# A two-block transformer kernel: the layout of on-chip memory, and short two-byte products behind the norms

## The chip, the cores and the metric

The kernel runs on one core of a Trainium2 chip. The metric is the device time of one launch in microseconds (us). A core has a matrix engine (PE, whose weight loads the profile lists apart as PEld), a vector engine (DVE), an activation engine (ACT), GpSimd (POOL) and a queue engine (SP) that here only issues transfers. All of them read and write one on-chip memory of 128 partitions. An address below is an offset inside a partition, in KiB; it is the same in every partition and comes from the built program.

A PE product has a stationary operand, loaded first, and a moving operand that streams past it. In the rows "128*128 128x256" is a product whose moving operand has 256 columns.

## The reference

256 tokens of width 1024 pass through two blocks, in float32:

```python
# block 1
h = rms_norm(x, g_mix); z = h @ w_in
x = x + concat(mla(...), hgrn2(...)) @ w_o
h = rms_norm(x, g_ffn)
x = x + (silu(h @ w_gate) * (h @ w_up)) @ w_down        # inner width 2816
x = x + sigmoid(rms_norm(x, g_ple) @ w_ple_gate) * (p @ w_ple_proj)
# block 2
proj = rms_norm(x, norm_mix_g) @ w_in_2                 # qa ka va qb kb vb f g_a g_b
ya = moba_attention(...) @ w_branch_a
yb = forgetting_attention(...) @ w_branch_b
x = x + (sigmoid(g_a) * ya + sigmoid(g_b) * yb) @ w_out
qh = rms_norm(x, norm_ffn_g) @ w_peer_q                 # 8 heads, two halves of 128
s = qh @ sub_keys; take the best 16 of 128 in each half, the best 16 of the 256 pairs, softmax
x = x + sum over the chosen of gate * gelu(h . expert_u[e]) * expert_v[e]   # 16384 experts
out = rms_norm(x, norm_final_g)
```

## The kernel before, in words

Activations lie transposed, features on partitions and 256 tokens along the row, in eight slices of 128 features. PE's accuracy on its fast float32r type does not do for float32, so every large product is made three times: an operand is split into a rounded part and a remainder (hh and hl for activations, whi and wlo for weights), and hi·hi, lo·hi and hi·lo are added up in PSUM. `mm3s` (L120 to L131) issues them for products that keep features on partitions: weights stationary, activations moving, 256 columns, all by the PE call of L129. `natural` (L163) does it with activations stationary and weights moving, 512 columns, for the projections that are wanted with tokens on partitions.

`unit` (L99 to L118) brings weights in: SP starts the transfer of a 512 KB piece into `wraw` (L108), ACT rounds it to `whi` (L109), DVE takes the difference `wlo` (L114). Each has four buffers.

A norm is spread over the products that follow it. Class `Norm` splits the unscaled residual times the gain into hh and hl, and `make` returns two steps that are placed between products: `sums` (L230 to L237) adds the squares of a token over the partitions by true float32 products against `ones` and has DVE (L197, tile nv) and POOL (L198, tile rnat) make the root; `spread` (L239 to L244) puts the root, by two more float32 products (L241), across the partitions, and ACT copies it to rbc. The results of the products are multiplied by it later. Where the products are 128 wide and the weights come in units, a step stands behind a unit's 24 products.

In block 2 the products `whole` (L1063) multiply 18 groups of 128 experts in true float32 straight from `wraw`, with `xf`, the normed activations, moving. The one-hot products (L1227) that turn chosen experts into a table of gates are float16, 128 columns, sixteen in a row. The last stage runs over 128 groups c of 128 experts: `prepare` brings in expert_v (whi, wlo), multiplies the hidden value by the gate (tile am) and splits it into `ah` and `al`; `multiply` (L1252) issues 12 products of 512 columns per group with ah or al stationary and whi or wlo moving, into four accumulators. While c is below 64 the hidden values of later groups (`experts_in`, L1066, 24 products of L129 each) run in between. Behind group 127 `final` adds the residual, squares, and scales the result per half j of the tokens.

Tiles come from pools. A name has a fixed number of buffers, and names of one pool lie one behind the other in the order of first use, so that the pools `res` (hh, hl, xa, xb, rnat, rbc) and `st` (wraw, whi, wlo, sq, sqa, nv) fill the memory from its low end, and pools of a stage come above them. PE's order is the program's order but for instructions that the scheduler may move; what follows is taken from the built program.

## Time and profile before

| | us |
|---|---|
| median of 3 runs | 1409.96 |
| lowest, highest | 1408.98, 1412.89 |
| the profiled execution | 1412.48 |
| span of the profiled execution (first to last instruction) | 1410.7 |

The span is cut into 40 slices, and PE is at 9 tenths or more in all but the last (7 tenths). PE's granted clock is 0.8 of full speed in the second slice and in the last, and 0.9 or more in all others. Transfers take 8 tenths of the DMA engines' time at most in a slice, 196 GB/s on the mean.

A view with a row for a group of instructions gives their count, the sum of their times and the mean time of one. Products on PE overlap: the next one starts before the last has ended, so the mean time of one is longer than the distance from start to start. That distance, called the pitch below, is what a product costs in a row of products. It is had from a stretch in which PE never stopped: the length of the stretch plus one duration, divided by the number of products in it.

### The profile page before, as it was taken

The numbers are of one execution on the slowest core, as the hardware profiler recorded it, in microseconds if no ns is written. First come the engines' busy times: TensorE is split into PE (matmuls) and PEld (weight loads), VectorE is DVE, ScalarE is ACT, GpSimd is POOL, SyncE is SP. The second block draws the span as 40 slices with busy tenths as digits, with TensorE's granted clock in tenths as the row PEclk, the third lists the DMA queues.
The fourth block names the chain that finished last, engine by engine and source line by source line (L and its number), as shares of the span: only waits on it lengthen the run. The fifth ranks groups of instructions, "written<-read, shape, count | busy, mean of one in ns | idle before, by whom it ended". The sixth has DMA issues, their size and how long they took to land.

```text
span 1410.7 us, 25321 instructions
## 1 busy us (share of the span) xinstructions
PE 1390.7 (99%) x9970; PEld 1275.8 (90%) x9970; DVE 966.8 (69%) x1794; ACT 766.5 (54%) x1183; POOL 127.0 (9%) x117
## 2 busy tenths in 40 slices
PE   9999999999999999999999999999999999999997
PEld 9896999999989889999999999999989989888885
DVE  7867876665675556897989975555555555577775
ACT  6765655444654444573368885554444444445443
POOL 4322100000110000147200000000000000000000
PEclk9899999999999999999999999999999999999998
DMA  8572566566555334676478779667767767787662
GB/s 244 163 190 62 162 197 187 187 180 187 176 165 153 117 120 135 196 212 189 134 235 285 275 271 297 210 214 211 224 194 222 219 210 227 225 278 237 196 192 77
DMA packets 104999, 276.99 MB, mean 196 GB/s; under 512 B 8496, under 2 KB 42032, under 8 KB 102704
## 3 DMA queue, kind: packets, MB, share of 16 engines
q1 hardware_dynamic: 100848, 252.31, 57.6%
q10 hardware_dynamic: 2304, 16.78, 2.9%
q0 software_dynamic: 1728, 6.29, 2.5%
q8 instruction: 78, 1.28, 0.4%
q14 instruction: 41, 0.34, 0.1%
HBM read 251.23 MB, written 17.83 MB: 191 GB/s over the span
## 4 chain that ended last, share of the span: by engine, by line
PE 91%; DVE 4%; ACT 2%; DMA 2%; issue 1%; POOL 1%; SPq 0%; POOLq 0%; ACTq 0%; DVEq 0%
PE mm L129 50%; PE ax L1252 25%; PE mm L163 4%; PE ax L1227 2%; PE mm L1063 1%; DVE wlo L114 1%; PE sc L923 1%; ACT whi L109 1%; PE sc L129 1%; PE ao L917 1%; PE ay L163 1%; DMA wraw<-in_expert_v_dram 1%; PE ax L1038 1%; DVE hl L186 0%; DMA wraw<-in_expert_u_dram 0%
## 5 line engine op out<-in xcount | busy, mean ns | idle before, releaser
L109 ACT ACTIVATE whi<-wraw 128x1024 fp32r<-128x1024 f32 (+3 forms) x446 | 457.4, 1031 | 471.1 <-PE mm L129 249.4
L114 DVE TENSOR_TENSOR wlo<-wraw,whi 128x1024 fp32r<-128x1024 f32 (+3 forms) x412 | 489.0, 1190 | 253.2 <-ACT whi L109 243.7
L129 PE MATMUL mm<-hh,whi 128*128 128x256 f32 x1920 | 278.4, 283 | 1.1 <-ACT hh L185 0.4
L129 PE MATMUL mm<-hl,whi 128*128 128x256 f32 x1920 | 268.7, 278 | 0.9 <-DVE hl L186 0.8
L129 PE MATMUL mm<-hh,wlo 128*128 128x256 f32 x1920 | 267.2, 278 | 0.2 <-DVE wlo L114 0.2
L129 PEld LDWEIGHTS mm<-hh,whi 128*128 128x128 f32 x1920 | 249.4, 188 | 9.1 <-issue 0.9
L129 PEld LDWEIGHTS mm<-hl,whi 128*128 128x128 f32 x1920 | 241.6, 188 | 2.3 <-DVE hl L186 2.1
L129 PEld LDWEIGHTS mm<-hh,wlo 128*128 128x128 f32 x1920 | 241.3, 188 | 0.5 <-DVE wlo L114 0.3
L1252 PE MATMUL ax<-whi,al 128*128 128x512 f32 x512 | 201.2, 396 | 0.0
L1252 PE MATMUL ax<-wlo,ah 128*128 128x512 f32 x512 | 200.5, 395 | 0.0
L1252 PE MATMUL ax<-whi,ah 128*128 128x512 f32 x512 | 200.4, 395 | 0.0
L1252 PEld LDWEIGHTS ax<-whi,ah 128*128 128x128 f32 x512 | 96.2, 188 | 22.0
L1252 PEld LDWEIGHTS ax<-wlo,ah 128*128 128x128 f32 x512 | 96.3, 188 | 21.2
L1252 PEld LDWEIGHTS ax<-whi,al 128*128 128x128 f32 x512 | 96.2, 188 | 20.6 <-DVE al L181 0.4
L1068 ACT ACTIVATE hs<-mm 128x256 f32<-128x256 f32 x128 | 47.4, 371 | 40.1 <-PE mm L129 25.8
L1267 POOL TENSOR_TENSOR ff<-fss 128x1 f32<-128x1 f32 x2 | 1.4, 698 | 718.9 <-ACT fsq L1262 718.9
L114 POOL TENSOR_TENSOR wlo<-wraw,whi 128x1024 fp32r<-128x1024 f32 x22 | 52.5, 2397 | 24.9 <-ACT whi L109 22.9
L180 ACT ACTIVATE ah<-am 128x256 fp32r<-128x256 f32 x128 | 51.5, 402 | 4.4 <-DVE am L1243 4.4
L181 DVE TENSOR_TENSOR al<-am,ah 128x256 fp32r<-128x256 f32 x128 | 53.3, 418 | 0.0
L786 DVE TENSOR_TENSOR gu<-mm,rbc 128x256 f32<-128x256 f32 x44 | 18.6, 424 | 39.4 <-PE mm L129 39.4
L1217 DVE TENSOR_TENSOR one<-iota,iab 128x2048 f16<-128x2048 f16 x32 | 39.1, 1220 | 4.1 <-PE ax L1227 4.1
L1220 DVE TENSOR_TENSOR oA<-one,g 128x2048 f16<-128x2048 f16 x32 | 39.1, 1225 | 1.0
(407 smaller groups left out, 1552.4 us busy)
## 6 DMA issues: line engine op xcount, KB each, us to landing
wraw<-in_expert_u_dram SPq DMA_DIRECT2D x128, 512.0 KB, 4.5
wraw<-in_expert_v_dram SPq DMA_DIRECT2D x128, 512.0 KB, 3.9
wraw<-in_w_gu_dram SPq DMA_DIRECT2D x44, 512.0 KB, 3.5
wraw<-in_w_in_nat_dram SPq DMA_DIRECT2D x24, 512.0 KB, 3.7
wraw<-in_w_down_dram SPq DMA_DIRECT2D x16, 512.0 KB, 3.5
wraw<-in_w_in_g_dram SPq DMA_DIRECT2D x16, 512.0 KB, 3.5
wraw<-in_w_pq_dram SPq DMA_DIRECT2D x16, 512.0 KB, 4.4
gd<-hh ACTq DMA_DIRECT2D x8, 1024.0 KB, 6.8
```

Source lines behind the costliest of these rows:

```text
L109: S.activation(hi[:, s], raw[:, s], AF.Copy)
L114: (G if pool else V).tensor_tensor(lo[:, s], raw[:, s], hi[:, s].bitcast(F32), op=OP.subtract)
L129: PE.matmul(o, (wh, wl, wh)[j], (xh, xh, xl)[j], start=first and n == 0, stop=last and n == len(order) - 1)
L163: PE.matmul(p, xs[:, x0 + k, s], w[:, k], start=first and i == 0 and k == 0, stop=last and i == 2 and k == kts - 1)
L180: S.activation(hi, src, AF.Copy)
L181: V.tensor_tensor(lo, src, hi.bitcast(F32), op=OP.subtract)
L786: V.tensor_tensor(t, o, n1.r, op=OP.mult)
L1068: S.activation(t, p[:, :T], AF.Gelu)
L1217: V.tensor_tensor(one, iota[:, None].to_broadcast(s2), iab[:, qs].rearrange("p q w b -> p (q w) b")[:, :, None].to_broadcast(s2), op=OP.is ...
L1220: V.tensor_tensor(A2, ow[:, :, 0:1].to_broadcast(s3), g2[:, qs].rearrange("p q k b -> p (q k) b")[:, :, None].to_broadcast([128, PAIRS * 2 ...
L1227: PE.matmul(p[:, i * 128:(i + 1) * 128], ow[:, q, 1, b::2], A2[:, q, k, b::2], start=k == 0, stop=k == 1)
L1252: PE.matmul(acc[j * 2 + n], (al, ah, ah)[i][:, j * 128:(j + 1) * 128], (hi, lo, hi)[i][:, n * 512:(n + 1) * 512], start=c == 0 and i == 0, ...
```

## The change

**Layout.** Two pools, `reh` and `sth`, are laid from the high end of the memory. The residual streams xa and xb, the roots rnat and rbc, the raw weights wraw, the squares and nv go there. So the split activations and weights move down, and with them everything above. `ah` and `al` become slices of one tile in a buffer of `hl` that is free by then, and the odd ones of the gate tiles `gt`, which used hl, get a tile of their own. In KiB of a partition, from the built programs:

| tile (use on PE) | before | after |
|---|---|---|
| hh (moving in L129, stationary in L163) | 27.9 to 43.9 | 20.1 to 36.1 |
| hl (the same) | 43.9 to 59.9 | 36.1 to 52.1 |
| whi (stationary in L129, moving in L163, L1252) | 85.9 to 101.9 | 52.1 to 68.1 |
| wlo (the same) | 101.9 to 117.9 | 68.1 to 84.1 |
| act high and low, moving in w_down | 122 to 166 | 84.1 to 128 |
| oT, moving in w_branch | 156 to 172 | 118 to 134 |
| ah, al (stationary in L1252) | 210 to 218 | 44.1 to 52.1 |
| xf, moving in L1063 | 124 to 132 | 86 to 94 |
| float16 one-hots (L1227) | 198 to 214 | 160 to 176 |
| wraw, stationary in L1063 | 69.9 to 85.9 | 185.8 to 201.8 |
| keys in xa's place, moving in L1038 | 19.9 up | 205.9 up |
| xb's place, stationary in a few products of L163 | 59.9 up | 213.9 up |

**Two-byte products.** `level` issues one bfloat16 product of 128 columns on a tile of ones, into a region of PSUM that nothing reads. It stands seven times in the program: behind `spread` in each of five norms, once in w_down behind the first 24 products, and once behind the products `whole`.

**A spread moved.** In the first block of w_in_2 the step `spread` stands one group of products later.

**The end.** In `final`, the sum, scaling and epsilon of the two halves' squares go from POOL to DVE, POOL keeps the power alone, and the two additions of the residual for the last half come behind one another.

```diff
+    reh = pool("reh", side="right")
+    sth = pool("sth", side="right")
...
-        raw = st.tile([128, 1024], F32, name="wraw", bufs=4)
+        raw = sth.tile([128, 1024], F32, name="wraw", bufs=4)
...
-                sq = st.tile([128, T], F32, name="sq", bufs=2)
+                sq = sth.tile([128, T], F32, name="sq", bufs=2)
...
             def spread():
                 for j in range(2):
                     PE.matmul(self.p[:, T + j * 128:T + (j + 1) * 128], self.rn[:, j:j + 1].to_broadcast([128, 128]), ident,
                               start=True, stop=True)
-                self.r = res.tile([128, T], F32, name="rbc", bufs=2)
+                level(self.p[:, 0:128])
+                self.r = reh.tile([128, T], F32, name="rbc", bufs=2)
                 S.activation(self.r, self.p[:, T:], AF.Copy)
...
-    xa = lambda: res.tile([128, 8, T], F32, name="xa")
-    xb = lambda: res.tile([128, 8, T], F32, name="xb")
+    xa = lambda: reh.tile([128, 8, T], F32, name="xa")
+    xb = lambda: reh.tile([128, 8, T], F32, name="xb")
...
+    onesb = con.tile([128, 128], BF16, name="onesb")
+    G.memset(onesb, 1.0)
+
+    def level(p):
+
+        tc.keep_in_program_order(PE.matmul(p, onesb, onesb, start=True, stop=True))
...
                      n == 0 and k1 == 22, first=k0 == 0, last=k1 == 22)
+                if n == 0 and k0 == 0:
+                    level(pfx()[:, 0:128])
...
-        nat512("w_in2_nat", 0, h, emit_nat("qa"), pre=[lambda: None] + nb.make(ppt), behind=nb.last)
+        fsum, fspread = nb.make(ppt)
+        nat512("w_in2_nat", 0, h, emit_nat("qa"), pre=[lambda: None, fsum, lambda: None, fspread], behind=nb.last)
...
         ahead(2, "whole")
+        level(pax()[:, 0:128])
...
+            parts = res.tile([128, 2 * LAST, T], F32R, name="hl", bufs=2)
...
-                ah = lv.tile([128, T], F32R, name="ah", bufs=LAST)
-                al = lv.tile([128, T], F32R, name="al", bufs=LAST)
+                ah = parts[:, 2 * (c % LAST)]
+                al = parts[:, 2 * (c % LAST) + 1]
...
             def final(j):
 
                 ss = lv.tile([128, 2], F32, name="fss", bufs=2)
+                f = [lv.tile([128, 1], F32, name=f"ff{i}", bufs=2) for i in range(3)]
                 for n in range(2):
                     ns = slice(n * 512, (n + 1) * 512)
                     V.tensor_tensor(xr[:, j, ns], xr[:, j, ns], acc[j * 2 + n], op=OP.add)
                     sq = lv.tile([128, 512], F32, name="fsq", bufs=1)
                     S.activation(sq, xr[:, j, ns], AF.Square, accum_out=ss[:, n:n + 1])
-                f = [lv.tile([128, 1], F32, name=f"ff{i}", bufs=2) for i in range(3)]
-                for n in range(2):
-                    ns = slice(n * 512, (n + 1) * 512)
-                    if n == 1:
-                        G.tensor_tensor(f[2], ss[:, 0:1], ss[:, 1:2], op=OP.add)
-                        rstd(f[0], f[1], f[2], 1.0 / D, G)
-                    V.tensor_tensor(xr[:, j, ns], xr[:, j, ns], fin[:, ns], op=OP.mult)
+                    if n == 0:
+                        V.tensor_scalar(f[1], ss[:, 0:1], 1.0 / D, EPS, op0=OP.mult, op1=OP.add)
+                        V.tensor_tensor(xr[:, j, ns], xr[:, j, ns], fin[:, ns], op=OP.mult)
+                V.scalar_tensor_tensor(f[2], ss[:, 1:2], 1.0 / D, f[1], op0=OP.mult, op1=OP.add)
+                G.tensor_tensor(f[0], f[2], mhalf, op=OP.pow)
+                tc.keep_in_program_order(V.tensor_tensor(xr[:, j, 512:], xr[:, j, 512:], fin[:, 512:], op=OP.mult))
...
-                    gt = res.tile([128, T // TBLK, CBLK, TBLK], F32, name="hh" if c // CBLK % 2 == 0 else "hl", bufs=2)
+                    shape = [128, T // TBLK, CBLK, TBLK]
+                    gt = res.tile(shape, F32, name="hh", bufs=2) if c // CBLK % 2 == 0 else lv.tile(shape, F32, name="gt")
```

On PE, at the spread of the norm ahead of the gate and up products (cst is the unit matrix; L129 and L241 of before are L132 and L244 of after). Before:

```order
L129 MATMUL mm<-hh,whi 128x256 x8
L129 MATMUL mm<-hl,whi 128x256 x8
L129 MATMUL mm<-hh,wlo 128x256 x8
L241 MATMUL fx<-cst,rnat 128x128 x2
L129 MATMUL mm<-hh,whi 128x256 x8
```

After:

```order
L132 MATMUL mm<-hh,whi 128x256 x8
L132 MATMUL mm<-hl,whi 128x256 x8
L132 MATMUL mm<-hh,wlo 128x256 x8
L244 MATMUL fx<-cst,rnat 128x128 x2
L278 LDWEIGHTS onesb
L278 MATMUL fx<-onesb 128x128
L132 MATMUL mm<-hh,whi 128x256 x8
```

The float32r products go on after a bfloat16 product instead of after the float32 products of the spread.

On PE, in the first block of w_in_2, from the last of the sums on. Before:

```order
L234 MATMUL pt<-ones,sq 128x128
L163 MATMUL mm<-whi,hh 128x512 x2
L163 MATMUL mm<-whi,hl 128x512 x2
L163 MATMUL mm<-wlo,hh 128x512 x2
L163 MATMUL mm<-whi,hh 128x512 x2
L163 MATMUL mm<-whi,hl 128x512 x2
L163 MATMUL mm<-wlo,hh 128x512 x2
L241 MATMUL pt<-cst,rnat 128x128 x2
L163 MATMUL mm<-whi,hh 128x512 x2
```

After, from the products of the next unit on, up to the products for the forget gate (32 partitions), which follow:

```order
L166 MATMUL mm<-whi,hh 128x512 x2
L166 MATMUL mm<-whi,hl 128x512 x2
L166 MATMUL mm<-wlo,hh 128x512 x2
L244 MATMUL pt<-cst,rnat 128x128 x2
L278 LDWEIGHTS onesb
L278 MATMUL pt<-onesb 128x128
L132 MATMUL mm<-hh,whi 32x256 x8
```

Twelve products of 512 columns that stood behind the spread now stand ahead of it.

On DVE, the end of the program, from the first addition for the last half on. Before:

```order
L1260 TENSOR_TENSOR xr<-xr,ax 128x512
L1269 TENSOR_TENSOR xr<-xr,fin 128x512
L1260 TENSOR_TENSOR xr<-xr,ax 128x512
L1269 TENSOR_TENSOR xr<-xr,fin 128x512
L1273 TENSOR_SCALAR xr<-xr,ff_16181 128x512
```

After:

```order
L1277 TENSOR_TENSOR xr<-xr,ax 128x512 x2
L1281 TENSOR_SCALAR ff_15938<-fss 128x1
L1282 TENSOR_TENSOR xr<-xr,fin 128x512
L1283 SCALAR_TENSOR_TENSOR ff_15939<-fss,ff_15938 128x1
L1285 TENSOR_TENSOR xr<-xr,fin 128x512
L1289 TENSOR_SCALAR xr<-xr,ff_15937 128x512
```

The second addition no longer stands behind the multiplication by the gain, which waits for ACT's square; two short operations on one column are new. Elsewhere the orders of the engines are the same in both programs but for what follows from these edits.

## Rows read from the trace of the kernel before

**Rows 1.** The page: busy time by engine; one line of the costliest groups

```profile
PE 1390.7 (99%) x9970; PEld 1275.8 (90%) x9970; DVE 966.8 (69%) x1794; ACT 766.5 (54%) x1183; POOL 127.0 (9%) x117
...
L129 PE MATMUL mm<-hh,whi 128*128 128x256 f32 x1920 | 278.4, 283 | 1.1 <-ACT hh L185 0.4
```

**Rows 2.** Windows, L129: stretch, us, busy time (count), granted clock, DMA share, GB/s

```profile
184.00:369.00 185.00, 185.00 (x1572) 184.97 (x1571) 1.00 0.62 188
376.00:390.00 14.00, 14.00 (x121) 14.00 (x120) 1.00 0.45 126
552.00:573.00 21.00, 21.00 (x181) 21.00 (x180) 1.00 0.58 177
576.00:597.00 21.00, 21.00 (x188) 21.00 (x186) 1.00 0.66 201
605.60:663.00 57.40, 54.22 (x432) 51.87 (x432) 1.00 0.68 201
```

**Rows 3.** Timeline, PE, at the spread ahead of gate and up: start, us, operation

```profile
179.24 1.07 PE L129 MATMUL mm<-hh,wlo 128*128 128x256 f32 x8
180.15 0.60 PE L241 MATMUL fx<-cst,rnat 128*128 128x128 f32 x4
180.51 1.19 PE L129 MATMUL mm<-hh,whi 128*128 128x256 f32 x8
181.53 1.10 PE L129 MATMUL mm<-hl,whi 128*128 128x256 f32 x8
```

**Rows 4.** Timeline, PE, around one group of one-hot products

```profile
736.64 1.09 PE L1227 MATMUL ax<-oA,one 128*128 128x128 f16 x16
737.54 1.18 PE L129 MATMUL mm<-hh,whi 128*128 128x256 f32 x8
738.56 1.07 PE L129 MATMUL mm<-hl,whi 128*128 128x256 f32 x8
```

**Rows 5.** Timeline, PE, where w_branch's products begin

```profile
550.47 1.07 PE L129 MATMUL mm<-hh,wlo 128*128 128x256 f32 x8
551.37 0.63 PE L129 MATMUL mm<-oTh,whi 128*128 128x256 f32 x4
```

**Rows 6.** Windows, L1252, the last stage; then timeline, PE, the ends of a row of L163

```profile
1225.00:1390.00 165.00, 165.00 (x708) 132.92 (x708) 1.00 0.70 219
...
410.10 0.62 PE L163 MATMUL mm<-wlo,hh 128*128 128x512 f32 x2
422.46 0.62 PE L163 MATMUL mm<-wlo,hh 128*128 128x512 f32 x2
```

**Rows 7.** Timeline, PE, DVE and POOL, at the spread in w_in_2

```profile
397.49 3.83 DVE L114 TENSOR_TENSOR wlo<-wraw,whi 128x1024 fp32r<-128x1024 f32 x4 [0.18 <-ACT whi L109]
400.27 0.62 PE L163 MATMUL mm<-wlo,hh 128*128 128x512 f32 x2
401.48 0.71 POOL L198 TENSOR_TENSOR rnat<-nv,mhalf 128x2 f32<-128x2 f32 x1 [4.06 <-DVE nv L197]
402.24 0.71 PE L241 MATMUL pt<-cst,rnat 128*128 128x128 f32 x4 [1.35 <-POOL rnat L198]
```

**Rows 8.** Timeline, all engines, the end

```profile
1400.31 1.09 PE L1252 MATMUL ax<-whi,ah 128*128 128x512 f32 x4
1400.89 0.68 DVE L1260 TENSOR_TENSOR xr<-xr,ax 128x512 f32<-128x512 f32 x1
1403.03 0.68 DVE L1260 TENSOR_TENSOR xr<-xr,ax 128x512 f32<-128x512 f32 x1
1403.80 0.63 ACT L1262 ACTIVATE fsq<-xr 128x512 f32<-128x512 f32 x1 [1.42 <-DVE xr L1260]
1405.66 0.56 POOL L198 TENSOR_TENSOR ff<-ff,mhalf 128x1 f32<-128x1 f32 x1
1406.25 0.48 DVE L1273 TENSOR_SCALAR xr<-xr,ff 128x512 f32<-128x512 f32 x1 [1.00 <-POOL ff L198]
```

**Rows 9.** Lines by form: true float32 products with xf moving

```profile
L1063 PE MATMUL mm<-xf,wraw 128*128 128x256 f32 x144 | 31.6, 379 | 0.0
```

More of the change, by code (lines that the diff above doesn't have):

```diff
@@ L221, in add @@
             else:
-                t = st.tile([128, T], F32, name="sqa", bufs=2)
+                t = sth.tile([128, T], F32, name="sqa", bufs=2)
                 G.tensor_tensor(t, self.parts[0], sq, op=OP.add)
@@ L234, in sums @@
                         PE.matmul(p[:, js], sq[:, js], ones, start=i == 0, stop=i == len(self.parts) - 1)
-                v = st.tile([128, 2], F32, name="nv", bufs=2)
-                self.rn = res.tile([128, 2], F32, name="rnat", bufs=2)
+                v = sth.tile([128, 2], F32, name="nv", bufs=2)
+                self.rn = reh.tile([128, 2], F32, name="rnat", bufs=2)
                 rstd(self.rn, v, p[:, 0:T:128], 1.0 / D)
@@ L1059, in experts_in @@
             if how == "whole":
-                raw = st.tile([128, 8, 128], F32, name="wraw", bufs=4)
+                raw = sth.tile([128, 8, 128], F32, name="wraw", bufs=4)
                 nc.sync.dma_start(raw, a["expert_u"][c])
@@ L1155, in body @@
             V.tensor_tensor(dsk[:, 1:], sk[0][:, 1:], sk[0][:, :-1], op=OP.subtract)
-            m1 = res.tile([128, 16, 256], BF16, name="xa")
+            m1 = reh.tile([128, 16, 256], BF16, name="xa")
             m2 = B16("lk", 16, 256)
```

## The prediction, made before the changed kernel ran

> **What bounds the kernel now.** I read the busy times by engine first: PE works 99% of the span, DVE 69%, ACT 54% [rows 1]. So nothing that another engine gains counts unless PE stands still there, and nearly all of the time is the number of products times their pitch. Next come the windows over stretches in which PE never stopped, since a mean duration of overlapping products hides the pitch: (stretch + one duration of 0.28 us) / count. With 256 columns this gives 185.28/1572 = 117.9 ns from the first gate product to the end of w_down, 14.28/121 = 118.0 in the gate of the third norm, 21.28/181 = 117.6 in w_branch and 21.28/188 = 113.2 in w_out [rows 2]. These are the same kind of product at the same granted clock of 1.00, the 2.4 GHz level. The DMA share is higher in the fast stretch (0.66 against 0.45 to 0.61), so transfers don't make the difference. There are **two pitches, 113.2 and 117.8**, and the gap, 4.6 ns, is 4% of a product.
>
> Then the timelines, to see where the pitch changes. (a) Ahead of the FFN the eight products behind the spread's float32 products take 1.19 us and the next eight 1.10, where eight ahead of it took 1.07 [rows 3]; the slow pitch then holds through all of gate, up and w_down. (b) Behind sixteen float16 products the first eight are slow too (1.18), but the next eight are back at 1.07 [rows 4]. So a return from float32 can leave PE in the slow pitch for good, and a return from a two-byte type leaves the fast one; the row is one of 32 such groups. (c) w_branch begins with no other type in between: only the moving operand goes from hh at 28 to 60 KiB to oT at 156 to 172, and four products then take 0.63 us [rows 5], pitch 117.6, until w_out, with hh again, runs at 113.2 [rows 2]. So an **operand's address** counts as well. (d) With 512 columns, products of L163, both operands low, go from 410.10 to 422.46 with 54 products in between: 12.36/54 = 228.9 ns. In the last stage, with ah and al at 210 to 218 stationary, 165.4/708 = 233.6 [rows 6].
>
> **The change part by part,** made against the profiled 1412.5 us (span 1410.7 and what lies around it).
>
> *Two-byte products.* Behind the spread of the second norm: 1056 gate and up products less the 24 ahead of it, 528 of w_down and 48 of the small projection, 1608, all in one unbroken slow stretch; at 4.6 ns, 7.4 us if one bfloat16 product does what sixteen float16 ones do [rows 2 to 4]. Behind the spread of the third norm 192 - 24 = 168 products: 0.8. The products of w_peer_q (432 counted in their stretch [rows 2]) have the float32 scores between them with no two-byte product behind, and the one behind the 18 whole groups comes just ahead of one-hot groups which do the same: I count 0 for both; if the layout helped the former, 432 x 4.6 = 2.0. The price: seven products of 128 columns, each at least 0.9/16 = 0.06 us as in the one-hot row, and up to 0.11 more for another return (1.18 against 1.07) [rows 4]. That is 0.4 to 1.2; I take 0.9, the upper end's side, since each stands alone.
>
> *Layout, what wins.* w_branch's oT moves to 118 to 134 and its weights to 52 to 84: 192 x 4.4 = 0.8 us if the low place is what counts; that oT is still 34 KiB above the weights leaves doubt, so 0 is the other end. In the last stage the stationary operand goes from 210 to 44 and the moving ones below 84, both within the span that L163 reads at 228.9. 128 x 12 = 1536 products; the full gap of 4.7 ns gives 7.2; half of them stand in groups of twelve behind products of another width, where I credit 3.8, an estimate: 3.6 + 2.9 = 6.5. Ends: 0, and, since 512 columns at twice the rest of a fast 256 would be 226.4, some 4 more.
>
> *Layout, what loses.* Operands that go high are wraw in the 144 true float32 products (379 ns each [rows 9], starts nearer together), the keys in the scores, and xb's few. No row has a float32 product from a high place. The nearest is the gap of 4.6 ns: 144 x 4.6 = 0.7, with keys and xb some 0.8; 0 at the other end. That act lies at 84 to 128 in w_down, not low, is the doubtful part of the 7.4: if it stays slow, 528 x 4.6 = 2.4 are lost.
>
> *The moved spread.* PE's products end near 400.73, the spread starts at 402.24 and 1.35 us are put down to POOL's root; DVE made the sum ready only behind four wlo of 3.83 us in a row [rows 7]. Twelve products of 512 columns, 12 x 0.229 = 2.7 us, now stand ahead of it, with their weights ready (the fourth wlo ends at 401.32, and the products that use it are the last of the twelve). The root is then there before it is wanted. Saved 1.2, between 0.5 (the next unit's weights come late instead) and 1.5. The forget-gate products behind it get their root later, but only their result needs it.
>
> *The end.* The last products start at 1400.31 and end at 1401.4. DVE's second addition starts at 1403.03, behind the multiplication that waits for ACT's square; then square, POOL's three steps, and the scaling at 1406.25 [rows 8]. After: additions at 1400.89 and 1401.57, the second square (0.63 and some 0.2 for its sum) behind the first until about 1403.2, a short DVE step, POOL's power of 0.56 and the scaling at about 1404.1. Saved 2.1, all on the path; from 1.6 to 2.5, as the multiplication of 0.68 falls ahead of the short step or not.
>
> *What a faster PE asks of others.* A unit of 24 products takes 2.72 instead of 2.83 us; DVE makes a wlo in 3.83/4 = 0.96 [rows 7] and transfers hold 0.61 of the DMA engines' time [rows 2], so nothing comes late. Other places of tiles change no wait on DVE, ACT or SP that PE feels; the odd gate tile now has one buffer, and its load is issued many groups ahead of use.
>
> Sum: 7.4 + 0.8 + 0.8 + 6.5 + 1.2 + 2.1 - 0.9 - 0.8 = 17.1 us, 1395.4 for the profiled execution. This stood 2.5 above the median, so **1393.0** on the median.
>
> **The rivals.** *A, the addresses count for nothing* beyond w_branch's own reasons: only the pitch behind the norms, the spread and the end stay, 7.4 + 0.8 + 1.2 + 2.1 - 0.9 = 10.6, 1399.4. Against it: (c) switches at the address alone. For it: 233.6 and 228.9 differ in more than an address.
>
> *B, one lone product doesn't bring the fast pitch back*; the rows show sixteen float16 ones, never one bfloat16. Then 0.8 + 6.5 + 1.2 + 2.1 - 0.9 - 0.8 = 8.9, 1401.1.
>
> *C, neither does anything*, because the pitch is set by what the trace doesn't show, such as the order of the weight loads: 1.2 + 2.1 - 0.9 = 2.4, 1407.6. The Trainium skill speaks for this: "TensorE: Matmul & The Clock Gate", section "Back-to-back issue gap", gives a product's gap from its columns alone, 2.5 ns over one column per cycle, about 109 and 216 ns here as an estimate, with no term for address or for what ran before; "SBUF — State Buffer" says that PE never waits on anyone there. By these pages the change could give only C. The trace doesn't agree: two values for one width and one clock [rows 2], both above the page's.
>
> *D, slower: neighbours collide.* Before, 26 KiB lie between hl's end and whi; after, they touch at 52.1. If a stationary and a moving operand close to each other are what makes the slow pitch, every stretch turns slow that is fast now, some 3,000 products (5760 from hh and hl [rows 1] less 1032, 168, 432 and an estimated thousand behind odd types): +13.8 - 2.4 = 11.4, 1421.4. With the gains of both mechanisms gone it decides from (2.4 + 4.2)/0.0046, some 1,400 products turned slow, on. Against it: w_out's operands lie nearer together than w_branch's and are the fast ones.
>
> **How the numbers follow.** The forecast (both mechanisms work, within some us) 0.60, A 0.13, B 0.14, C 0.08, D 0.05. The range: the forecast's own with the doubtful terms down to 0 (2.4 of w_down, 0.8, about 3 of the last stage, 0.7 of the spread, 0.5 of the end: 7.4) reaches 1400.4, with the hopeful ones (2.0 of w_peer_q, 4 of the last stage, 0.8 of the losses, and about 1 of the rest) 1385; A and B need 1401 and their own doubts some us more: 1385 to 1405. A measurement of this kernel tells 0.3%, 4.2 us, from no change, so faster means below 1405.7. The forecast, A and B lie there: faster 0.87, same 0.08 (C), slower 0.05 (D).
>
> **What would show it.** Right: the gate and up stretch at 113.2 (some 1060 products in 120 us), w_branch at 113, the last stage at 229 or less, no stop of PE at the moved spread, and 2.8 us from the last product's end to the scaling, not 4.85. If gate and up stay at 117.8, B; if the last stage stays at 233.6 or w_branch at 117.6, A; if w_out or the products among the one-hot groups turn to 117.8, D. w_down alone at 117.8 would say that act is still too high.

## The result: 1428.5 us, slower by 1.0%

The changed kernel takes 1428.49 us (median of 4 runs, 1427.89 to 1429.47), the kernel before 1411.43 beside it (1408.98 to 1416.01). The ratio is 1.0097, with a 95% interval from 1.0069 to 1.0124. The forecast was 1393.0, so not only the size is wrong, but the sign.

PE is as busy as it was (99%) with seven products more, so the 16 us between the two spans (1427.0 against 1410.7) are in the products themselves. The page of the changed kernel, first part, answers [rows 1]:

```profile
PE 1409.3 (99%) x9977; PEld 1303.4 (91%) x9977; DVE 967.6 (68%) x1798; ACT 768.1 (54%) x1183; POOL 125.9 (9%) x114
```

Windows of the changed kernel, L132 (before: L129), as in [rows 2]: from the first gate product into w_down, the gate of the third norm, w_branch, w_out; and then the last stage, L1268 (before: L1252), as in [rows 6]:

```profile
184.00:369.00 185.00, 185.00 (x1543) 184.95 (x1542) 1.00 0.60 184
378.50:392.00 13.50, 13.50 (x114) 13.50 (x114) 1.00 0.49 160
558.00:579.00 21.00, 21.00 (x177) 21.00 (x177) 1.00 0.56 168
583.00:606.00 23.00, 23.00 (x194) 23.00 (x193) 1.00 0.58 183
...
1250.00:1405.00 155.00, 155.00 (x686) 128.38 (x685) 1.00 0.74 230
```

The same reading as before, (stretch + 0.28)/count, gives 185.28/1543 = 120.1 ns, 21.28/177 = 120.2 and 23.28/194 = 120.0. So every 256-column product of these rows, the fast ones of before as well, now takes **120 ns**, a third pitch, slower than both known ones. The 512-column products, of which one lasts 0.39 us, went the other way: 155.39/686 = 226.5 against 233.6.

Added up from the start-to-start distances in the two traces: some 6300 products of 256 columns in unbroken rows took 730.0 us before (115.64 ns each) and take 756.2 (119.77), 26.2 more; everything at 512 columns, with the waits between, took 446.0 and takes 434.7, 11.3 less; other products and waits make some 3 more. The last product starts at 1419.2 instead of 1401.0. The end gives back 2.1.

Two terms of the sum came out. The timeline of the changed kernel at the moved spread, PE, has no stop left [rows 7]:

```profile
407.38 0.61 PE L166 MATMUL mm<-wlo,hh 128*128 128x512 f32 x2
407.84 0.61 PE L244 MATMUL pt<-cst,rnat 128*128 128x128 f32 x4
408.28 0.22 PE L278 MATMUL pt<-onesb 128*128 128x128 bf16 x1
408.31 1.10 PE L132 MATMUL mm<-hh,whi 128*32 128x256 f32 x8
409.25 1.07 PE L132 MATMUL mm<-hl,whi 128*32 128x256 f32 x8
```

And its end, all engines, against [rows 8]:

```profile
1418.48 1.07 PE L1268 MATMUL ax<-whi,hl 128*128 128x512 f32 x4
1418.77 1.50 DVE L1277 TENSOR_TENSOR xr<-xr,ax 128x512 f32<-128x512 f32 x2
...
1421.12 0.16 DVE L1283 SCALAR_TENSOR_TENSOR ff<-fss,ff 128x1 f32<-128x1 f32 x1
1421.36 0.94 POOL L1284 TENSOR_TENSOR ff<-ff,mhalf 128x1 f32<-128x1 f32 x1 [3.03 <-DVE ff L1283]
1422.34 0.49 DVE L1289 TENSOR_SCALAR xr<-xr,ff 128x512 f32<-128x512 f32 x1 [0.46 <-POOL ff L1284]
```

From the end of the last products (1419.55) to the scaling it is 2.79 us, where 4.85 had been. From the first product of the spread to the next float32r product it is 0.47 us (407.84 to 408.31), where it was 0.36 without a bfloat16 product (180.15 to 180.51 in [rows 3]).

One line there is a first hint at the cause: the forget gate's products, with the same hh and hl but only 32 stationary columns ("128*32"), run eight in 1.07 us, the fast pitch, in the middle of a kernel whose other 256-column products are slow. Their slices of the weights lie 128 bytes apart, not 512, so the type, the moving operands and the clock are not what makes the others slow.

### The profile page after: what moved, and what is told of

It is laid out like the page before. It is cut to its first block, busy times and chain, and to the rows that moved or that the text cites. A ratio compares the mean times of both kernels' runs of the same rounds, so it can differ in the third digit from the quotient of the medians.

```text
span 1427.0 us, 25343 instructions
## 1 busy us (share of the span) xinstructions
PE 1409.3 (99%) x9977; PEld 1303.4 (91%) x9977; DVE 967.6 (68%) x1798; ACT 768.1 (54%) x1183; POOL 125.9 (9%) x114
## 4 chain that ended last, share of the span: by engine, by line
PE 89%; DVE 5%; DMA 2%; ACT 2%; issue 1%; POOL 0%; SPq 0%; POOLq 0%; ACTq 0%; DVEq 0%
PE mm L132 49%; PE ax L1268 24%; PE mm L166 4%; PE ax L1242 2%; PE mm L1077 1%; DVE hl L189 1%; DVE wlo L117 1%; PE sc L936 1%; PE sc L132 1%; ACT whi L112 1%; PE ao L930 1%; PE ay L166 1%; DMA gd<-hl 1%; DMA hh<-gd 0%; DMA wraw<-in_expert_u_dram 0%
## 5 line engine op out<-in xcount | busy, mean ns | idle before, releaser
L1268 PE MATMUL ax<-whi,hl 128*128 128x512 f32 x1024 | 322.3, 391 | 0.0
L132 PE MATMUL mm<-hh,whi 128*128 128x256 f32 x1920 | 284.2, 286 | 0.7 <-ACT hs L1082 0.6
L132 PE MATMUL mm<-hl,whi 128*128 128x256 f32 x1920 | 278.0, 283 | 0.8 <-DVE hl L189 0.7
L132 PE MATMUL mm<-hh,wlo 128*128 128x256 f32 x1920 | 276.2, 283 | 0.4 <-DMA wlo<-wraw 0.4
L132 PEld LDWEIGHTS mm<-hh,whi 128*128 128x128 f32 x1920 | 253.7, 190 | 7.6 <-ACT hs L1082 0.8
L132 PEld LDWEIGHTS mm<-hl,whi 128*128 128x128 f32 x1920 | 250.7, 192 | 1.6 <-DVE hl L189 1.4
L132 PEld LDWEIGHTS mm<-hh,wlo 128*128 128x128 f32 x1920 | 250.5, 192 | 0.6 <-DMA wlo<-wraw 0.6
L1268 PEld LDWEIGHTS ax<-whi,hl 128*128 128x128 f32 x1024 | 190.9, 188 | 38.3 <-DVE hl L184 0.5
L1268 PE MATMUL ax<-wlo,hl 128*128 128x512 f32 x512 | 197.7, 390 | 0.0
L1268 PEld LDWEIGHTS ax<-wlo,hl 128*128 128x128 f32 x512 | 96.3, 188 | 18.6
L183 ACT ACTIVATE hl<-am 128x256 fp32r<-128x256 f32 x128 | 51.5, 402 | 6.0 <-DVE am L1259 6.0
L184 DVE TENSOR_TENSOR hl<-am,hl 128x256 fp32r<-128x256 f32 x128 | 53.3, 418 | 0.0
L1242 PE MATMUL ax<-oA,one 128*128 128x128 f16 x512 | 34.9, 219 | 0.8 <-DVE oA L1235 0.8
L166 PE MATMUL mm<-whi,hh 128*128 128x512 f32 (+1 forms) x112 | 34.4, 393 | 0.0
```

The costliest lines, as they stand in the source:

```text
L132: PE.matmul(o, (wh, wl, wh)[j], (xh, xh, xl)[j], start=first and n == 0, stop=last and n == len(order) - 1)
L166: PE.matmul(p, xs[:, x0 + k, s], w[:, k], start=first and i == 0 and k == 0, stop=last and i == 2 and k == kts - 1)
L183: S.activation(hi, src, AF.Copy)
L184: V.tensor_tensor(lo, src, hi.bitcast(F32), op=OP.subtract)
L1242: PE.matmul(p[:, i * 128:(i + 1) * 128], ow[:, q, 1, b::2], A2[:, q, k, b::2], start=k == 0, stop=k == 1)
L1268: PE.matmul(acc[j * 2 + n], (al, ah, ah)[i][:, j * 128:(j + 1) * 128], (hi, lo, hi)[i][:, n * 512:(n + 1) * 512], start=c == 0 and i == 0, ...
```

## The experiments

The built programs give the addresses to the byte. The table of KiB hid this: in the kernel before, hh and hl start at 128 modulo 256 bytes, whi and wlo at 192, act, oT, ah and al at 0; in the changed one all of these start at 128. Let the **shift** be the stationary operand's address less the moving one's, modulo 256.

| | hh, hl with weights (256 columns) | act, oT with weights (256) | ah, al with weights (512, last stage) |
|---|---|---|---|
| before | 64 | 192 | 64 |
| changed | 0 | 0 | 0 |
| + 64 bytes (first experiment) | 64 | 64 | 192 |
| before, + 64 bytes | 128 | 0 | 0 |
| changed, fitted | 64 | 64 | 0 |
| before, two pads (and the two versions built on it) | 64 | 64 | 0 |

Three theories stood against each other: alignment (the shift sets the pitch), place (the KiB do, which the prediction had taken for granted, in its layout terms and in its rival D), and what ran before (a two-byte product sets a pitch that lasts, fast as forecast or, as it now could be, slow).

### A bench for the pitch alone

Shortened from the bench's source, with comments added; there are 50 pairs of addresses:

```diff
+for kind, m, s in segments():          # 50 pairs of addresses
+    float32(4); stream(kind, m, s)     # 48 float32r products, k = 0..7: moving m + 1024 k, stationary s + 512 k
+    short(half, 16); stream(kind, m, s)
```

> A bench for the pitch alone: the transformer is left out, the output is the input copied. Rows of 48 float32r products over one large tile, the moving operand stepping 1024 bytes and the stationary one 512 bytes per product as in the kernel, for 51 pairs of start addresses: the stationary one moved by 0 to 448 bytes, the moving one by 32 to 448 bytes, either one put at other KiB; behind each return from float32 and behind each return from sixteen float16 products. Theory 1 (alignment: the two operands' addresses modulo a small power of two decide whether the two streams meet): the 256-column pitch changes between about 113 and 120 ns with the shift in bytes, repeats with it, and is the same at every KiB for the same shift. Theory 2 (place: the KiB decide): the pitch doesn't change with the shift and changes between 52, 68, 88, 120, 160 and 184 KiB. Theory 3 (what ran before decides): the rows behind float32 differ from those behind float16 at the same addresses.

Timeline of the bench, PE (L78 float32, L83 two-byte, L91 256 columns, L93 512 columns). First moving 28 KiB, stationary 88 KiB at shift 0, and at shift 64 behind float32 and behind float16; then stationary 52 KiB at shift 0 and 64; stationary 184 KiB at 0 and 64; moving 156 KiB at 0 and 64; then 512 columns at shift 0, 64, 128, 192:

```profile
29.47 5.99 PE L91 MATMUL mm<-big 128*128 128x256 f32 x48
106.26 5.90 PE L91 MATMUL mm<-big 128*128 128x256 f32 x48
112.88 5.70 PE L91 MATMUL mm<-big 128*128 128x256 f32 x48
...
373.02 5.99 PE L91 MATMUL mm<-big 128*128 128x256 f32 x48
385.92 5.70 PE L91 MATMUL mm<-big 128*128 128x256 f32 x48
473.89 5.99 PE L91 MATMUL mm<-big 128*128 128x256 f32 x48
486.79 5.70 PE L91 MATMUL mm<-big 128*128 128x256 f32 x48
524.33 5.99 PE L91 MATMUL mm<-big 128*128 128x256 f32 x48
537.23 5.70 PE L91 MATMUL mm<-big 128*128 128x256 f32 x48
...
549.55 11.17 PE L93 MATMUL mm<-big 128*128 128x512 f32 x48
596.61 11.45 PE L93 MATMUL mm<-big 128*128 128x512 f32 x48
620.42 11.39 PE L93 MATMUL mm<-big 128*128 128x512 f32 x48
644.11 11.25 PE L93 MATMUL mm<-big 128*128 128x512 f32 x48
```

A row of 48 takes 5.99 us at shift 0 and 5.70 at shift 64, whether the stationary operand lies at 52, 88 or 184 KiB or the moving one at 156. The place counts for nothing. As means of the start-to-start distance over the last 35 products of a row:

| shift, bytes | 256 columns, ns | 512 columns, ns |
|---|---|---|
| 0 | 120.0 (all 22 rows) | 226.7 |
| 64 | 113.3 (21 rows) or 117.8 (3 rows) | 233.3 |
| 128 | 118.7 (4 rows) or 120.0 (4 rows) | 232.4 |
| 192 | 117.8 (all 18 rows) | 228.9 |
| others (4 to 48, 96, 160, 224) | 115.6 to 123.1 | 233.3 (at 32) |

The shift repeats with 256: 320 behaves as 64, 256 as 0. The table has all pitches of both kernels: 117.8 in w_branch and w_down before (192), 228.9 in L163 before (192: here the weights move), 233.3 in the last stage before (64), 120.0 and 226.7 in the changed kernel (0). At shift 64 there are two values at one pair of addresses: the row at 106.26 is slow, the one at 112.88 fast. Two values at one pair are seen at shift 128 too (118.7 and 120.0), and at 16, 48 and 224; but 113.3 is seen at 64 alone.

### The changed kernel with weights 64 bytes further

Comments added:

```diff
+    padw = st.tile([128, 16], F32, name="padw")     # ahead of whi and wlo
...
+        padz = st.tile([128, 112], F32, name="padz")  # behind them, so that all else stands as it did modulo 512
```

> The changed kernel with a pad of 64 bytes ahead of whi and wlo and one of 448 behind them, so that the weights stand 64 bytes off the activations modulo 128, as in the kernel before, and everything else keeps its place modulo 512. Theory 1 (alignment): the 6400 products of 256 columns leave 119.75 ns for 113 to 117.8, which takes 12 to 41 us off: 1387 to 1416. Theory 2 (place): no change, 1428. Theory 3 (the two-byte products put PE into the slow pitch): no change, 1428.

1407.6 us (1405.98 to 1409.44, 10 runs), 0.9953 of the kernel before (0.9928 to 0.9979). So **64 bytes take 21 us off** the changed kernel, with all of its low places and its seven products. Windows, L134: gate and up, w_down, w_branch; then L1272, the last stage:

```profile
190.00:290.00 100.00, 100.00 (x852) 100.00 (x851) 1.00 0.59 186
310.00:355.00 45.00, 45.00 (x400) 45.00 (x399) 1.00 0.69 198
552.00:568.00 16.00, 16.00 (x143) 16.00 (x142) 1.00 0.54 173
...
1225.00:1385.00 160.00, 160.00 (x701) 131.29 (x700) 1.00 0.72 228
```

100.28/852 = 117.7, 45.28/400 = 113.2, 16.28/143 = 113.8 (113.3 from the distances), and 160.39/701 = 228.8: the bench's values for shifts 64 and 192. Gate and up stand behind two float32 products and a bfloat16 one and have the slower of the two values at shift 64; w_down, at the same shift and next in the same row, has the faster. Between them stands the one two-byte product that is alone among float32r products, in w_down behind the first 24. The timeline of this kernel, PE, there:

```profile
300.93 1.10 PE L134 MATMUL mm<-acth,wlo 128*128 128x256 f32 x8
301.88 0.23 PE L280 MATMUL fx<-onesb 128*128 128x128 bf16 x1
301.92 1.18 PE L134 MATMUL mm<-acth,whi 128*128 128x256 f32 x8
302.93 1.07 PE L134 MATMUL mm<-actl,whi 128*128 128x256 f32 x8
```

From start to start it is 117.8 ns over the 1031 recorded products ahead of it and 113.5 over the 540 behind. The fitted version below, the other trace with this product at shift 64, has the same (117.8 and 113.4). So a lone two-byte product was followed by the fast pitch in both, as the prediction wanted it; in the changed kernel the shift of 0 leaves no fast pitch to return to.

### The kernel before with weights 64 bytes further

```diff
     st = pool("st")
+    padw = st.tile([128, 16], F32, name="padw")
...
         unit0 = unit(a["w_in"][0], (8, 128), parts=4, between=load_x)
+        padz = st.tile([128, 112], F32, name="padz")
```

> The kernel before with the same two pads, so that weights and activations stand alike modulo 128. Theory 1 (alignment): 256 columns go from 115.65 to 120 ns on the mean, 6400 x 4.1 = 26 us more, about 1437; 512 columns may win. Theory 2 (place): as before, 1410. Theory 3: as before, 1410.

1429.02 us in the only run (by the distances some 24 us more at 256 columns, where 26 were expected, and 9 less at 512), 17.6 over the kernel before beside it (1411.39): **the changed kernel's loss, from 64 bytes alone**. The expectation took the shift modulo 128; by the bench's period of 256, hh stands at 128 and not at 0 here. Windows, L131, gate and up and then w_down, and L1256, the last stage:

```profile
190.00:290.00 100.00, 100.00 (x835) 100.00 (x835) 1.00 0.59 182
310.00:360.00 50.00, 50.00 (x419) 50.00 (x418) 1.00 0.62 186
...
1250.00:1400.00 150.00, 150.00 (x664) 124.24 (x663) 1.00 0.72 229
```

120.1 and 120.0 for shifts 128 and 0, and 150.39/664 = 226.5 for 512 columns at 0. Alignment holds; place and what ran before, which both expected 1410, don't.

### The two-byte products alone, and the change without them

The first adds only the seven products to the kernel before, the second takes only them out of the changed one.

```diff
+                level(self.p[:, 0:128])          # behind spread; likewise in w_down and behind the 18 whole groups
```

> The kernel before with the seven two-byte products alone. As predicted (a lone bfloat16 product gives the fast pitch back): the gate, up and w_down products go from 117.8 to 113.3, 1411 - 7.4 - 0.8 + 0.9 = 1404. Rival B: they stay at 117.8, 1412. Theory 3 (the two-byte products put PE into the slow pitch): 120 in all stretches behind them, 1425 or more.

1415.8 us against 1411.39, ratio 1.0013 (0.9986 to 1.0040): no gain clear of noise, and the expected 1404 is outside. Gate and up behind the spread's two float32 products and a bfloat16 one, L129:

```profile
190.00:290.00 100.00, 100.00 (x851) 100.00 (x850) 1.00 0.59 184
```

117.8 ns, so in this execution a two-byte product behind two float32 ones did not bring the fast pitch back. In w_down, at shift 192 here, the lone one changes nothing (117.8 ahead of it and behind it). (The tile of ones takes 256 bytes, so all tiles above it move by 256 together, and the shifts are those of before.)

```diff
-                level(self.p[:, 0:128])
...
-                    level(pfx()[:, 0:128])
...
-        level(pax()[:, 0:128])
```

> The changed kernel without its seven two-byte products. If they are worth nothing: 256 columns stay at 120 ns and the time at 1428. If they had any part in the slow pitch: fewer than 119.75 ns on the mean, below 1424.

1425.66 us, one run. Windows, L132, gate and up:

```profile
190.00:290.00 100.00, 100.00 (x836) 100.00 (x835) 1.00 0.59 184
```

100.28/836 = 120.0, and 119.74 on the mean of all products. The two-byte products have no part in the slow pitch.

### What picks the pitch at shift 64

Shortened from the bench's source:

```diff
+for again in range(2):
+    for kind, n in RETURNS:            # ten kinds of interruption
+        for u in ALIGN:                # the pair at 0, 64, ... 448 modulo 512, shift 64
+            interruption(kind, n); stream(256, 28 * K + u, 88 * K + u + 64, 24)
```

> A bench again, the transformer left out, the output is the input copied. Rows of 24 float32r products of 256 columns whose stationary operand stands 64 bytes above the moving one modulo 256, the only shift at which both 113.3 and 117.8 ns were seen. Ten kinds of interruption ahead of a row (2, 4 or 6 float32 products, 1, 4 or 16 float16 ones, a bfloat16 one, four float32 and a bfloat16 one, one float32r product of 64 or of 512 columns), each at eight alignments of the pair modulo 512, and the whole set twice. Theory 1 (the kind of what ran before decides): all rows behind one kind are alike, 113.3 behind two-byte types. Theory 2 (the addresses modulo 512 decide): all rows of one alignment are alike. Theory 3 (the moment at which the row is entered decides): both pitches occur behind every kind and at every alignment, and the second set agrees with the first only where what runs ahead took the same time.

(A float32 product is two records in the trace; what the expectation calls 2, 4 and 6 are records, that is one, two and three products.) The timeline of the bench, PE, behind two float32 products, at alignments 192 and 256:

```profile
32.41 2.99 PE L75 MATMUL mm<-big 128*128 128x256 f32 x24
35.24 0.61 PE L62 MATMUL ex<-ones 128*128 128x128 f32 x4
35.60 3.07 PE L75 MATMUL mm<-big 128*128 128x256 f32 x24
```

Rows at 117.8, of 16 behind each kind: one float32 product 0, two 6, three 0; one float16 product 0, four 8, sixteen 6; one bfloat16 product 0, two float32 and then one bfloat16 product 12; one float32r product of 64 columns 6, of 512 columns 10. Every row settles in the one or the other value and keeps it. No alignment sets it by itself, and the type does not either: one or three float32 products leave only fast rows, two leave both kinds. But four of the ten kinds have no slow row at all, where theory 3 wanted both pitches behind every kind. The second set repeats the first in 78 of 80 rows; the two others stand behind two float32 products, the kind that comes first and so has other work ahead of it the first time. What the rows show is that the work just ahead picks the pitch; that it does so by the moment of entry is the likeliest reading, not shown. The combination "two float32, one bfloat16", which is what the changed kernel does behind each spread, was the worst of the ten.

Next, no edit at all: the kernel before, profiled a second time.

> The kernel before, unchanged, profiled once more. If the pitch at shift 64 is chosen by the moment of entry, some stretches of gate and up, w_peer_q, the one-hot groups or the last norm's products show the other pitch than in the first profile, and the stretches at other shifts (w_down and w_branch at 117.8, the last stage at 233.3) the same one. If the program alone decides, every stretch shows the same pitch as before.

The kernel before, unchanged, windows, L129, gate and up and then w_down:

```profile
190.00:290.00 100.00, 100.00 (x885) 100.00 (x884) 1.00 0.64 197
310.00:360.00 50.00, 50.00 (x427) 50.00 (x426) 1.00 0.63 193
```

100.28/885 = 113.3 where [rows 2] had 117.9, in the same program: gate and up enter either pitch from one execution to the next. W_down, at shift 192, is at 117.8 in both. Of the long rows gate and up are the only one that differs; the third norm's gate and w_peer_q, at shift 64 too, are at 117.8 in both profiles.

The pitch is not all that differs. This execution took 1415.47 us, 3.0 more than the first one that was profiled, though its gate and up took 4.5 less. Windows, PE, in the first profile and in this one:

```profile
117.00:123.00 6.00, 5.99 (x29) 1.00 0.14 45
117.00:123.00 6.00, 6.00 (x13) 0.50 0.14 49
```

The granted clock is at 1.00, the 2.4 GHz level, in the one and at 0.50, the 1.2 GHz level, in the other, after a stretch from 110 to 117 in which PE was busy for 5.5 us in both. With a second such stretch earlier (0.83 on the mean of 5 to 15 us, 1.00 in the first profile), the spread ahead of gate and up starts at 186.32 instead of 180.15 [rows 3]. Of the 69 runs of the kernel before beside the experiments, the 15 with a mean granted clock of 0.992 or less have a median of 1418.2 us, the 15 with 0.995 or more one of 1411.1: the scatter of a kernel's runs is the clock's as well as the pitch's.

Then the kernel before with a third float32 product in `spread`:

```diff
+                tc.keep_in_program_order(PE.matmul(self.p[:, 0:128], self.rn[:, 0:1].to_broadcast([128, 128]), ident,
+                                                   start=True, stop=True))
```

> The kernel before with the third float32 product behind each spread and nothing else. If an odd count sets the fast pitch: gate and up products at 113.3 instead of 117.8, 1056 x 4.4 = 4.6 us off, w_down still at 117.8 (its moving operand stands at shift 192): 1405 to 1409 against 1411. If the entry is set by something else: as before, 1411 to 1412.

1415.66 us against 1413.63, ratio 1.0019 (0.9998 to 1.0040). The odd count, which was always fast in the bench, brings no gain in time, and the expected 1405 to 1409 is missed. In the profiled execution gate and up were fast (885 in 100 us), but so they were in the unchanged kernel above; the version with the third product below settles it.

### Versions that beat both

The changed kernel with its weights 64 bytes further, and the parts at shift 0 to them:

```diff
-            parts = res.tile([128, 2 * LAST, T], F32R, name="hl", bufs=2)
+            padv = lv.tile([128, 16], F32, name="padv")
+            parts = lv.tile([128, 2 * LAST, T], F32R, name="parts")
```

> The changed kernel with weights 64 bytes off the activations modulo 256 for the 256-column products, as in the run with the two pads, and in the last stage the split gate values alike with the weights modulo 256 (a tile of their own with a pad of 64 bytes ahead; the odd gate tiles go back to the buffer they had before). Theory alignment: 1536 products of 512 columns go from 229.0 to 226.7 ns, 3.6 us off the run with the two pads: 1404. Theory place: as that run, 1407.6; or, since the split values lie high again, 233 ns and 1414.

1407.82 us, ratio 0.9952 (0.9932 to 0.9972). The last stage, L1274, high again at 159 KiB but at shift 0:

```profile
1225.00:1380.00 155.00, 155.00 (x686) 128.34 (x685) 1.00 0.75 234
```

155.39/686 = 226.5: place is out a second time. The expected 3.6 us don't show in the time. In this kernel's trace the 1536 products of `experts_in` that stand between groups of 512 columns all entered slow (117.76 ns), where the kernel with the 64 bytes alone had 115.61 on their mean: 1536 x 2.15 = 3.3 us, which takes the gain back.

The kernel before with act, oT and what follows moved to shift 64, and ah and al to shift 0:

```diff
+        padz = st.tile([128, 32], F32, name="padz")
...
+            padv = lv.tile([128, 16], F32, name="padv")
```

> The kernel before with two pads and nothing else: 128 bytes behind the split weights, so that act, oT and the other moving operands above stand at the same shift from the weights as hh (64 modulo 256 instead of 192), and 64 bytes ahead of ah and al, so that these stand alike with the weights modulo 256. Theory alignment: the last stage goes from 233 to 226.7, 1536 x 6.3 = 9.7 us off; w_branch and w_down can reach 113.3, 192 x 4.4 + 528 x 4.4 = 3.2 more: 1398 to 1402 against 1411. Theory place: no change, 1411.

1406.56 us (1399.50 to 1411.59), ratio 0.9939 (0.9913 to 0.9964), in the old layout. Windows, L129, w_down and w_branch; L1256, the last stage:

```profile
310.00:353.00 43.00, 43.00 (x382) 43.00 (x381) 1.00 0.67 197
548.00:566.00 18.00, 18.00 (x162) 18.00 (x161) 1.00 0.59 178
...
1225.00:1380.00 155.00, 155.00 (x685) 128.39 (x684) 1.00 0.73 230
```

113.3, 112.8 (113.3 from the distances) and 226.8: 192 bytes of pads in a partition do what the change wanted from its layout. It falls short of the expected 1398 to 1402, since the products of `experts_in` enter slow here too. Windows, L129, over 47 of their 64 rows, in the kernel before and in this one:

```profile
960.00:1220.00 260.00, 136.06 (x1128) 135.37 (x1127) 1.00 0.70 214
960.00:1220.00 260.00, 140.50 (x1128) 139.59 (x1128) 1.00 0.69 214
```

That is 4.4 us more for the same products, and over all 64 rows 114.1 against 117.8 ns from start to start, 1536 x 3.6 = 5.5 us. Here the entry does not change from execution to execution. Among the traces with these rows at shift 64, 60 of the 64 rows are fast in each of the four with the last stage at shift 64 too, none in the four with it at shift 0, 40 in the one with it at 192. So the gain of the last stage, 1536 x 6.6 = 10.1 us, cost about half of itself in the 256-column products that stand between its groups, and the expectation had left that out.

Two pads, the third product, and the change's end and moved spread together:

```diff
+        padz = st.tile([128, 32], F32, name="padz")
...
+                tc.keep_in_program_order(PE.matmul(self.p[:, 0:128], self.rn[:, 0:1].to_broadcast([128, 128]), ident,
...
+        nat512("w_in2_nat", 0, h, emit_nat("qa"), pre=[lambda: None, fsum, lambda: None, fspread], behind=nb.last)
...
+            padv = lv.tile([128, 16], F32, name="padv")
...
+                G.tensor_tensor(f[0], f[2], mhalf, op=OP.pow)
```

> The kernel before with the two pads of the earlier run (1406.56 there), the changed kernel's end and its moved spread, and in each norm a third float32 product behind the two of the spread, in place of the bfloat16 one. Behind an odd count of float32 products the bench always showed 113.3 ns, behind two it showed either pitch. If that holds here: gate, up, the third norm's gate and w_out's neighbours at 113.3 in every execution, so that 2.1 (the end) and 0.6 to 1.5 (the spread) come off and the upper half of the run's scatter (1399.5 to 1411.6) goes: 1396 to 1403, less scatter. If the entry is set by something else here: about 1403 with the same scatter.

1408.61 us, ratio 0.9954 (0.9933 to 0.9975). Its 12 runs fall into two groups, five from 1401.41 to 1403.29 and seven from 1408.60 to 1412.58. The profiled execution is one of the second (1409.89). Gate and up, then w_down, L129, behind three float32 products:

```profile
190.00:290.00 100.00, 100.00 (x852) 100.00 (x851) 1.00 0.60 185
310.00:355.00 45.00, 45.00 (x385) 45.00 (x384) 1.00 0.63 191
```

117.7 and 117.6: the third product does not hold the fast pitch, and the time is above both expectations. The distance between the groups is near what 1608 products gain at the other pitch, 1608 x 4.5 = 7.2 us, and the mean granted clock (0.994 to 0.997) is the same in both; but no execution of the faster group was profiled, so that the pitch makes the groups is argued, not shown.

And the same without the third product:

```diff
-                tc.keep_in_program_order(PE.matmul(self.p[:, 0:128], self.rn[:, 0:1].to_broadcast([128, 128]), ident,
-                                                   start=True, stop=True))
```

> The kernel with the two pads, the changed end and the moved spread, without any added product. If the third float32 product of the last version was worth nothing (its profile had gate and up at 117.8), the time is that of the two pads less 2.1 for the end and 1.7 for the spread: 1402 to 1405, and it still falls into groups about 7 us apart, after the pitch that gate, up and w_down happen to enter with (1608 x 4.4 = 7.1). If the third product did help in most executions: 1407 or more.

**1404.0 us, ratio 0.9909 (0.9875 to 0.9944)**, three runs from 1399.97 to 1400.66 and three from 1407.34 to 1413.99. The time is as expected. It has the lowest ratio of the kernels tried, though the interval overlaps that of the two pads alone. The profiled execution is the slowest run: gate, up and w_down are at 117.8 ns (851 products in 100 us), and its mean granted clock is 0.990, against 0.995 to 0.997 in the other five.

## Why the prediction was wrong, point by point

**The reading of pitches.** That PE's time is products times pitch, that there were two pitches at the same clock, and that both an address and an entry from other work matter, all holds. The sizes that were worked out for the places in question, 4.6 ns and 4.7 ns a product, are near those of the bench (117.8 - 113.3 = 4.5, 233.3 - 228.9 = 4.4). The DMA share of the slow stretches goes up to 0.62 in [rows 2], not 0.61; nothing rests on it.

**The step that failed: from "an operand's address counts" to "the low place counts".** The two observations under (c) and (d) differ in the KiB, and in the low bits as well: oT stands at 0 modulo 256 and hh at 128, ah at 0 and hh at 128. The argument saw only the first difference. Told apart, the shift modulo 256 goes with every pitch seen here, but for the choice between two at shift 64, and the KiB explain none. The layout was then counted as a gain of 0.8 + 6.5 us, when it had moved all the large operands to the same 128 modulo 256. For 512 columns shift 0 is the best of those tried, by luck: 512-column products won 11.3 us, the moved spread's 1.7 among them, more than forecast. For 256 columns it is the worst of the steps of 64, and 26.2 us went there.

**The step on two-byte products.** "A return from float32 can leave PE in the slow pitch for good" was right for this one execution and no rule: the next execution of the same program had gate and up at 113.3. A profile is one draw where two pitches are possible. The 7.4 us were counted as a certain loss of before; for gate and up they are a loss of some executions, and the two-byte product behind the two float32 ones of a spread doesn't cure it (ratio 1.0013 alone, gate and up at 117.8 ns in the three traces that have it at shift 64). What the prediction took from sixteen float16 products held where one bfloat16 product stood alone among float32r products at shift 64 (117.8 to 113.5 ns), which is not where it had counted the gain. For w_down of before it could not have helped at all, as act at shift 192 was slow in every row.

**The rivals.** D had the sign and about the size (1421.4), with 0.05, and for a wrong reason: not neighbours in KiB, but alike in the low bits; operands at 28 and 184 KiB do the same. Its evidence against, that w_out's operands lie near each other and are fast, stands. B was right for the product behind a spread and not for the lone one in w_down, and its 1401.1 rested on the layout, like the rest. C's mechanism, a pitch set by what the trace doesn't show, was nearest to the truth: the address to the byte is in the built program, and no row has it. By the Trainium skill ("TensorE: Matmul & The Clock Gate", section "Back-to-back issue gap") the gap of a single 256-column product is about 109 ns, an estimate from its formula, which has no term for an address. The trace has 113.3, 117.8 and 120.0 for it at one clock.

**The small terms.** The end: 2.1 forecast, 4.85 - 2.79 = 2.1 measured, in part by luck: POOL's power took 0.94 us and not 0.56, and the additions began 0.78 us ahead of the last product's end (1418.77 to 1419.55), where before it was 0.51. The moved spread: 1.2 forecast; from the first product behind the sums to the forget gate it was 8.05 us (397.51 to 405.56) and is 6.34 (401.97 to 408.31), 1.7. The two-byte products' price: 0.9 forecast, 7 x (0.47 - 0.36) = 0.8 by the distance behind a spread. The true float32 products from a high place: 0.7 forecast, nothing measured (215.9 ns from start to start in both traces). None of them matters beside 26.2.

**What stays open.** The runs show that the shift sets the pitch and with what period, not what in the memory or in PE it meets. Nor do they show what in the work ahead of a row picks 113.3 or 117.8 at shift 64, or how to hold the fast one in the kernel. Of the kinds that were always fast in the bench, three float32 products failed there; one bfloat16 product between float32r products held in both traces that have it at shift 64, but no version has it ahead of gate and up. No shift was found at which 256 columns are always at 113.3.

## What to carry to other kernels

Where PE is the bound and operands fill whole rows of products, take the addresses of stationary and moving operand to the byte from the built program, and look at their difference modulo 256: here 64 bytes more between activations and weights were worth 21 us of 1428, and a new layout that looked only at KiB lost 17. Products of different width want different shifts (64 for 256 columns, 0 for 512), so an operand that serves both has to be put where more of the time is; and a faster pitch of the one kind can make the other enter slow, as `experts_in` did. And before a difference between two stretches of one profile is read as a rule, profile the same program twice.

## What the runs showed of the hardware that was not expected

- The start-to-start distance of float32r products of 256 columns with 128 stationary columns was 113.3, 117.8, 118.7 or 120.0 ns at the full clock at differences of the two operands' addresses that are multiples of 64 bytes, and that of 512 columns 226.7, 228.9, 232.4 or 233.3. It went with that difference modulo 256, not with the KiB.
- With 32 stationary columns and shifts 0 and 128 in turn, the forget gate's products ran at the fast pitch (eight in 1.07 us). They are not always there: with shifts 64 and 192 in turn their mean was 113.7 ns in the kernel before and 116.6 in the changed kernel with the 64 bytes.
- At shift 64 there are two lasting pitches at one pair of addresses; an unbroken row from gate to w_down kept the one that it entered with, 113.4 ns with the two pads and 117.8 in the two versions built on it, and the same program entered gate and up at either in two executions. Two groups of runs some 7 us apart fit this, while the changed kernel, at shift 0 in these rows, repeats within 1.6 us.
- At the same shift the products of `experts_in` took the same entry in every trace of one layout: fast in 60 of 64 rows behind 512-column products at 233.3 ns, slow in all 64 behind such products at 226.7.
